# Loads of the first modulation, the entry into attention, and sums behind it, in a two-layer streaming encoder

## The chip, the cores and the metric

The kernel is one program on one core of a Trainium2 chip. A core has TensorE (matmuls, results into PSUM banks), VectorE (DVE in the profile), ScalarE (ACT), GpSimd (POOL) and SyncE (SP, which only issues transfers here), each with its own queue of instructions that run in order, and 16 DMA engines that move data between HBM and the on-chip memory. Transfers are issued from the queues of SP, ACT and POOL. The metric is the device time of one execution in microseconds; lower is better.

## The reference

One inference step of a two-layer encoder on 1024 prompt tokens and 8 samples of 16 tokens, width 1024, float32. All tokens are handled as one batch of 1152 columns; data lie feature-major (128 partitions x 8 feature groups x tokens).

```
mod = silu(c) @ w_ada[l] + b_ada[l]                 # six parts: shift, scale, gate, twice
h   = rms_norm(x, norm_mix[l]) * (1 + scale) + shift
layer 0: RWKV-7 time mixing of h
   xr, xw, xk, xv, xa, xg = h + (h_prev - h) * mix[0..5]
   decay from tanh(xw @ w1) @ w2;  a from (xa @ a1) @ a2;  g from sigmoid(xg @ g1) @ g2
   recurrent state per head over time, group norm, bonus, times g, then @ w_o
layer 1: attention over bands of 9 chunks of 64, shared keys and values made after layer 0,
   q = rms_norm(h @ wb_q) per head;  softmax(q k / 8 + bias[relative distance]);  @ wb_o
each layer then: x = x + gate * SwiGLU(rms_norm(x) * (1 + scale) + shift)
```

Returned are the outputs, the shifted rows and states of layer 0, and the new keys and values.

## The kernel before, in words

Instructions are emitted by Python generators, and a planner of the tile framework then orders them for each engine: it simulates the time line with its own costs, keeps data dependencies and the tiles' reuse, and writes a fixed order per engine and per transfer queue. A tile belongs to a tag with a number of buffers; asking for one more than there are makes the next writer wait until an earlier one is released. `issue_after(ins)` puts the instructions of a block that run on the engine of `ins` behind `ins` in that order. Nearly every product is made in two parts for accuracy: `split` (L271 to L273) writes a rounded high part on ACT and the remainder on DVE, and `mm3` issues three matmuls, high x high, high x low and low x high.

*Beginning.* `setup` loads parameters and constants. `win_open` (L748) opens the pool of the recurrent part, loads the small table `T` (L753), and fills two scratch arrays `Z` in HBM with zeros (L760, four transfers). `proj(0)` (L522) then makes the first block of 384 tokens (408 columns with the shifted rows): `proj_h` (L432) loads the block `hb` (L434), sums squares over the 8 feature groups (ACT L439, DVE L441), forms `rstd` and multiplies (DVE L454), and scales and shifts each feature on ACT (L455). Scale and shift come from `ada_steps` (L201): a unit is four loads of 128 x 1024 weights (`wload`, L260), 16 matmuls on 32-wide quarters of the array, a copy (L222), four small matmuls and an addition (L228). Units 0 and 2 serve features 0 to 3, units 1 and 3 features 4 to 7; `proj_h` runs 8 steps, two units, before features 0 and 4. The weights go to tiles of the recurrent part that are still unused. The list `early` has 14 of them (YL, BKT, UV and XL three each, BK, pa); the 16 loads and the 4 copies of the sums take them in turn, twice round. After all eight features L462 clears column 0 of the block.

Then come the products of `proj_lora` (L574). The first, `wa1`, runs 48 matmuls: all eight features of the current rows, then all eight of the previous rows. Its weights are loaded on POOL's queue and mixed on DVE (`lora_weights`, L390 and L392); the two mixed tiles are also stored to HBM for the later blocks (L396, issued from ACT). They sit in tag `raw`, which has three buffers and also serves `g1a`, the next product.

*Attention.* `kv` makes keys and values and the first two of eight queries (`head`); in the second, scratch comes from `slot(1)`, a ring of 14 buffers of 1280 columns that holds much else. `attention` (L1634) goes over eight pairs of heads. For pair n the generator `queries(n + 2)` (L1720) loads the query weights in halves (L249, raw data in `slot(1)`), splits them and makes a query in four parts, woven between the score tiles; `pair` (L1734) first prepares keys and queries of pair n + 1 (`kprep` L1624, `qprep` L1631), then loads values and bias (L1744). `head_norm` uses two tiles of tag `ht` for each part, of five buffers. Output of two score tiles is copied from PSUM into tile `o`, one buffer (L1833), and stored (L1834).

*Projection behind attention.* `attproj` (L1910) multiplies by `wo` in eight steps of 640 columns, and between the steps `strassen_in` (L1286) prepares the first 512 columns of the feed-forward part: normed features, splits, and 16 sums or differences of 128 x 256 (L1299), which run on GpSimd here.

Of the kernel before, what the change touches and what calls it, by code (L numbers as in the profile page):

```python
# [8 lines left out]
F32 = mybir.dt.float32  # L9
# [136 lines left out]
class Trunk:  # L146
# [54 lines left out]
    def ada_steps(self, units, tag="aux", bufs=1, tile=None):  # L201
# [3 lines left out]
        def load(u, i):  # L205
            w = (tile or self.rawtile)()
            self.wload(w[:, :1024], self.a["wada"][u, i])
            return w
        todo = [(u, i) for u in units for i in range(4)]
        ahead = None  # L210
        for u in units:
            ps = self.bank(tag, bufs)
            for i in range(4):
# [3 lines left out]
                for q in range(4):  # L217
                    mm(nc, ps[32 * q:32 * q + 32, c], self.scT[:, i % 2 * 4 + q, :], w[:, q * 256:q * 256 + 256], i % 2 == 0, i % 2 == 1)
                if i < 3:
                    yield  # L220
            sb = (tile or self.rawtile)()[:, :512]
# [37 lines left out]
    def wload(self, out, src):  # L259
        (self.wqueue or self.nc.sync).dma_start(out, src)  # L260
# [120 lines left out]
    def lora_weights(self, n):  # L381
# [12 lines left out]
        for t in (raw, m):  # L394
            dt = self.dp.tile([128, c], F32, name=self.nm("lw"))
            nc.scalar.dma_start(dt, t[:, :c])  # L396
# [35 lines left out]
    def proj_h(self, b):  # L432
# [15 lines left out]
        for f in range(8):  # L448
# [6 lines left out]
            nc.scalar.activation(x[:, :n], x[:, :n], AF.Identity, scale=self.A0[f][:, 0:1], bias=self.mod[:, f, 0:1])  # L455
            if b == 2:
# [4 lines left out]
        if b == 0:  # L461
            nc.vector.memset(hb[:, :, 0:1], 0.0)  # L462
# [59 lines left out]
    def proj(self, b):  # L522

        if b == 0:
            self.lw = {}
            ring = (f() for _ in range(2) for f in self.early)
            self.ada = self.ada_steps((0, 2, 1, 3), "acc", 2, lambda: next(ring))
            self.A0 = [self.cp.tile([128, 9], F32, name=f"A0_{f}") for f in range(8)]
            self.proj_h(0)
            self.wqueue = self.nc.gpsimd  # L530
# [43 lines left out]
    def proj_lora(self, b, hi, lo):  # L574
# [5 lines left out]
        def first(n, rows):  # L580
            pw = self.bank("acc", 2)
            W = self.lora_in(n)
            for i, (h, l) in enumerate(((hc, lc), (hp, lp))):
                for k in range(8):
                    s = slice(k * rows, (k + 1) * rows)
                    self.mm3(pw[:rows, :TB], W[i][0][:, s], W[i][1][:, s], h[k], l[k], i + k == 0, i + k == 8)
# [161 lines left out]
    def win_open(self, ctx):  # L748
# [4 lines left out]
        nc.sync.dma_start(self.T.rearrange("p c i -> p (c i)"), self.a["ti"])  # L753
        self.Z = [self.dp.tile([64, 32, 64], F32, name=f"Z{i}") for i in range(2)]
        z = self.wt("y", [128, 512])
        nc.gpsimd.memset(z, 0.0)
        for i in range(2):
            zf = self.Z[i].rearrange("c g i -> (c g i)").rearrange("(u p x) -> u p x", u=2, p=128)
            for u in range(2):
                nc.sync.dma_start(zf[u], z)  # L760
        f4 = lambda t: t.rearrange("p a b c d -> p (a b c d)")
        f3 = lambda t: t.rearrange("p a b c -> p (a b c)")
        self.early = [lambda: f4(self.wt("YL", [128, 2, 2, 4, 64], 3))] * 3 + [lambda: f3(self.wt("BKT", [128, 2, 2, 256], 3))] * 3 + \
# [802 lines left out]
    def kv(self, H, X, end):  # L1566
# [40 lines left out]
        for n in range(2):  # L1607
            if n:
                self.evt = lambda tag: self.slot(1)
# [376 lines left out]
```

## Time and profile before

| quantity | value |
|---|---|
| time, median of three runs | 3811.97 us (3804.54 to 3815.72) |
| the profiled execution's own time | 3804.49 us |
| its span | 3802.7 us |
| TensorE busy, weight loads | 3506.1 us, 3098.0 us |
| VectorE, ScalarE, GpSimd busy | 2263.6, 1573.8, 591.6 us |
| mean granted TensorE clock | 0.94 |
| moved by DMA | 554.01 MB, 146 GB/s on average |

All times in the views are microseconds from the start of the span. A row of a time line gives start, duration, engine, line, operation, output and inputs, and in brackets the idle time ahead of it and what ended it. A row of waits gives total, count and longest. A row of groups gives busy time, mean nanoseconds of one, and the idle time ahead. A row of stretches gives, for each engine, busy time and number of instructions, then the granted clock, the DMA share and GB/s. The wide multiplications have one line, L143; they are told apart by their output: `acc`, `S`, `PT` and `O` are banks of PSUM.

### The profile page before, as it was taken

The page shows a single profiled execution, that of the slowest core. Times are in us where ns is not written, and L with a number is a line of the kernel's source. Part 1 is how long each engine was busy: PE and PEld are TensorE (multiplying, and loading weights), DVE is VectorE, ACT ScalarE, POOL GpSimd, SP SyncE. Part 2 cuts the span into 40 slices and gives each one's busy share as a digit, 9 for nine tenths or more (in the row PEclk, how much of TensorE's full clock was granted, in tenths as well). Part 3 has the DMA queues.
Part 4 walks back from the last instruction along what each step waited for, and adds up shares of the span by engine and source line. Part 5 has one row for each costly group of instructions (what it writes and reads, how often), then busy time and mean ns, then how long its engine had stood idle before and what let it go on. Part 6 is the DMA issues. An engine that isn't in the chain of part 4 may idle for free.

```text
span 3802.7 us, 72100 instructions
## 1 busy us (share of the span) xinstructions
PE 3506.1 (92%) x28550; PEld 3098.0 (81%) x28550; DVE 2263.6 (60%) x4396; ACT 1573.8 (41%) x3006; POOL 591.6 (16%) x497
## 2 busy tenths in 40 slices
PE   5889989989999799999999899789889799999999
PEld 4777778777667699999888879667677799999898
DVE  4666667765445854554457742666565755545667
ACT  5545546544223533333311452556554533333310
POOL 0000000000011154453000100000000255444000
PEclk9887899899699899999999999899899899999999
DMA  5876776776665322224654122554565322222521
GB/s 212 236 216 170 207 220 184 201 203 201 192 197 176 113 84 76 76 73 157 221 177 172 64 71 92 153 151 155 152 203 178 120 78 71 76 75 96 171 86 66
DMA packets 426995, 554.01 MB, mean 146 GB/s; under 512 B 128385, under 2 KB 292737, under 8 KB 422177
## 3 DMA queue, kind: packets, MB, share of 16 engines
q1 hardware_dynamic: 351344, 450.68, 36.9%
q0 software_dynamic: 22224, 80.36, 6.9%
q10 hardware_dynamic: 53088, 18.36, 2.1%
q8 instruction: 225, 3.69, 0.4%
q14 instruction: 114, 0.93, 0.1%
HBM read 415.85 MB, written 133.40 MB: 144 GB/s over the span
## 4 chain that ended last, share of the span: by engine, by line
PE 69%; DMA 11%; DVE 10%; issue 4%; ACT 4%; SPq 1%; ACTq 0%; POOL 0%; DVEq 0%; POOLq 0%
PE S L143 32%; PE PT L143 15%; PE acc L143 12%; PE st L143 3%; PE O L143 2%; PE G L143 1%; DVE h L273 1%; PE aux L143 1%; PE PT L1811 1%; PE Y L143 1%; DMA TT<-Z 1%; DMA h<-out_kT 1%; DVE wlo L273 1%; DMA raw<-in_rw_o 1%; DMA h<-in_wo 1%
## 5 line engine op out<-in xcount | busy, mean ns | idle before, releaser
L143 PE MATMUL S<-h,w 128*128 128x320 f32 (+1 forms) x4944 | 689.7, 298 | 12.3 <-ACT h L272 4.8
L143 PEld LDWEIGHTS S<-h,w 128*128 128x128 f32 x4944 | 671.8, 191 | 18.4 <-ACT h L272 5.6
L143 PE MATMUL S<-h,wh 128*128 128x320 f32 (+1 forms) x2844 | 529.8, 338 | 15.9 <-DVE h L1170 6.8
L143 PE MATMUL acc<-mx,whi 128*128 128x384 f32 x1728 | 508.5, 372 | 32.7 <-ACT whi L272 13.0
L143 PEld LDWEIGHTS S<-h,wh 128*128 128x128 f32 x2844 | 456.1, 189 | 70.8 <-issue 12.3
L272 ACT ACTIVATE w<-rq 128x512 fp32r<-128x512 f32 x308 | 192.6, 629 | 515.1 <-PE S L143 201.1
L143 PEld LDWEIGHTS acc<-mx,whi 128*128 128x128 f32 x1728 | 337.6, 204 | 63.3 <-ACT whi L272 16.9
L273 DVE TENSOR_TENSOR w<-rq,w 128x512 fp32r<-128x512 f32 x308 | 267.8, 872 | 199.8 <-ACT w L272 199.0
L143 PE MATMUL PT<-h,w 128*128 128x320 f32 (+1 forms) x2448 | 347.6, 297 | 10.2 <-ACT h L272 4.7
L143 PEld LDWEIGHTS PT<-h,w 128*128 128x128 f32 x2448 | 332.1, 190 | 12.2 <-ACT h L272 5.1
L143 PE MATMUL acc<-mx,wlo 128*128 128x384 f32 x864 | 316.1, 366 | 8.3 <-DVE wlo L273 8.3
L1369 POOL TENSOR_TENSOR t<-t,t 128x576 f32<-128x576 f32 (+1 forms) x132 | 226.5, 1717 | 442.2 <-ACT t L1376 320.1
L143 PE MATMUL PT<-h,wh 128*128 128x320 f32 (+1 forms) x1428 | 284.2, 342 | 8.2 <-ACT h L1558 2.3
L143 PEld LDWEIGHTS PT<-h,wh 128*128 128x128 f32 x1428 | 231.7, 188 | 38.5 <-issue 5.0
L143 PEld LDWEIGHTS acc<-mx,wlo 128*128 128x128 f32 x864 | 175.0, 203 | 20.6 <-DVE wlo L273 12.9
L273 DVE TENSOR_TENSOR wlo<-raw,whi 128x1024 fp32r<-128x1024 f32 x114 | 139.1, 1221 | 84.9 <-ACT whi L272 83.8
L272 ACT ACTIVATE wh<-rq 128x512 fp32r<-128x512 f32 x124 | 74.8, 625 | 245.1 <-PE S L143 161.4
L273 DVE TENSOR_TENSOR h<-h,h 128x1024 fp32r<-128x1024 f32 (+4 forms) x112 | 122.3, 1106 | 88.3 <-ACT h L272 72.1
L272 ACT ACTIVATE whi<-raw 128x1024 fp32r<-128x1024 f32 x114 | 119.6, 1053 | 129.0 <-PE acc L143 62.6
L272 ACT ACTIVATE h<-h 128x1024 fp32r<-128x1024 f32 (+4 forms) x112 | 103.5, 935 | 159.8 <-DMA h<-sd 111.1
L1369 DVE TENSOR_TENSOR t<-S,t 128x576 f32<-128x576 f32 (+1 forms) x116 | 86.4, 744 | 122.7 <-PE S L143 122.7
L1436 DVE TENSOR_TENSOR h<-h,S 128x640 f32<-128x640 f32 (+1 forms) x150 | 111.9, 750 | 78.9 <-PE S L143 78.7
(444 smaller groups left out, 5625.0 us busy)
## 6 DMA issues: line engine op xcount, KB each, us to landing
h<-in_wada SPq DMA_DIRECT2D x64, 512.0 KB, 6.3
rq<-in_wg SPq DMA_DIRECT2D x88, 256.0 KB, 2.6
rq<-in_wu SPq DMA_DIRECT2D x88, 256.0 KB, 2.6
rq<-in_wd SPq DMA_DIRECT2D x88, 256.0 KB, 3.1
raw<-in_wada POOLq DMA_DIRECT2D x32, 512.0 KB, 5.0
kc<-in_ck SPq DMA_DIRECT2D x16, 1024.0 KB, 5.1
vc<-in_cv SPq DMA_DIRECT2D x16, 1024.0 KB, 6.0
sd<-t SPq DMA_DIRECT2D x88, 160.0 KB, 1.9
```

Source lines behind the costliest of these rows:

```text
L143: return nc.tensor.matmul(out, lhsT, rhs, start=start, stop=stop)
L272: self.nc.scalar.activation(hi, x, AF.Copy)
L273: self.nc.vector.tensor_tensor(lo, x, hi, ALU.subtract)
L1369: eng.tensor_tensor(out, x, y, ALU.add)
L1436: nc.vector.tensor_tensor(y, y, d, ALU.add)
L1811: nc.tensor.transpose(pt[:, j * 128:(j + 1) * 128], P[:, j * 128:(j + 1) * 128], self.C("ident"))
```

## The change

In the beginning, the zero fill of `Z` and the load of `T` move into a new function `win_fill`, called after `proj_h(0)` and put behind the last modulation load on SP. Every modulation load has a tile, or two half tiles, of its own: the list `early` becomes an iterator over 12 full tiles of the old tags, two pairs of half tiles (tails of the XL tiles, and `gl`) and the tiles BK and pa; the copies of the sums go to four tiles TT. The two stores of `wa1`'s mixed weights are issued from SP behind the last modulation load, no longer from ACT. Column 0 is cleared feature by feature, and `wa1` of the first block takes features 0 to 3 of current and previous rows first, then features 4 to 7.

In attention, the weights of the third query are loaded in one transfer ahead of the second query's work and split in `queries(2)`; the ACT instructions of `kprep` and `qprep` in `pair` stand behind that split. Output copies take tiles of tag `ht`, which has six buffers in place of five; tag `o` is gone. In `attproj` the 16 sums run on VectorE.

```diff
@@ -198,14 +198,18 @@
             next(self.ada, None)

-    def ada_steps(self, units, tag="aux", bufs=1, tile=None):
+    def ada_steps(self, units, tag="aux", bufs=1, tile=None, sbt=None):

         nc = self.nc

         def load(u, i):
             w = (tile or self.rawtile)()
-            self.wload(w[:, :1024], self.a["wada"][u, i])
-            return w
+            if not isinstance(w, tuple):
+                w = w[:, :1024],
+            n = 1024 // len(w)
+            for j, t in enumerate(w):
+                self.last_load = self.wload(t, self.a["wada"][u, i][:, j * n:(j + 1) * n])
+            return [t[:, o:o + 256] for t in w for o in range(0, n, 256)]
         todo = [(u, i) for u in units for i in range(4)]
@@ -215,10 +219,10 @@
                 c = slice(i // 2 * 256, i // 2 * 256 + 256)
                 for q in range(4):
-                    mm(nc, ps[32 * q:32 * q + 32, c], self.scT[:, i % 2 * 4 + q, :], w[:, q * 256:q * 256 + 256], i % 2 == 0, i % 2 == 1)
+                    mm(nc, ps[32 * q:32 * q + 32, c], self.scT[:, i % 2 * 4 + q, :], w[q], i % 2 == 0, i % 2 == 1)
                 if i < 3:
                     yield
-            sb = (tile or self.rawtile)()[:, :512]
+            sb = sbt() if tile else self.rawtile()[:, :512]
             nc.scalar.activation(sb, ps, AF.Copy)
@@ -257,7 +261,7 @@

     def wload(self, out, src):
-        (self.wqueue or self.nc.sync).dma_start(out, src)
+        return (self.wqueue or self.nc.sync).dma_start(out, src)

@@ -393,7 +397,11 @@
         for t in (raw, m):
             dt = self.dp.tile([128, c], F32, name=self.nm("lw"))
-            nc.scalar.dma_start(dt, t[:, :c])
+            if n == "wa1":
+                with self.tc.issue_after(self.last_load.ins):
+                    nc.sync.dma_start(dt, t[:, :c])
+            else:
+                nc.scalar.dma_start(dt, t[:, :c])
             self.lw[n].append(dt)
@@ -453,13 +461,13 @@
             nc.vector.tensor_tensor(x, x, r, ALU.mult)
             nc.scalar.activation(x[:, :n], x[:, :n], AF.Identity, scale=self.A0[f][:, 0:1], bias=self.mod[:, f, 0:1])
+            if b == 0:
+                nc.vector.memset(x[:, 0:1], 0.0)
             if b == 2:
                 xs = x[:, n:].rearrange("p (b n) -> p b n", n=17)
                 bc = lambda t: t.rearrange("p (b o) -> p b o", o=1).broadcast_to([128, 8, 17])
                 nc.vector.tensor_tensor(xs, xs, bc(self.A0[f][:, 1:9]), ALU.mult)
                 nc.vector.tensor_tensor(xs, xs, bc(self.mod[:, f, 1:9]), ALU.add)
-        if b == 0:
-            nc.vector.memset(hb[:, :, 0:1], 0.0)
         if b == 2:
@@ -523,10 +531,11 @@
         if b == 0:
             self.lw = {}
-            ring = (f() for _ in range(2) for f in self.early)
-            self.ada = self.ada_steps((0, 2, 1, 3), "acc", 2, lambda: next(ring))
+            self.ada = self.ada_steps((0, 2, 1, 3), "acc", 2, lambda: next(self.early), lambda: next(self.early_sb))
             self.A0 = [self.cp.tile([128, 9], F32, name=f"A0_{f}") for f in range(8)]
             self.proj_h(0)
+            with self.tc.issue_after(self.last_load.ins):
+                self.win_fill()
             self.wqueue = self.nc.gpsimd
@@ -580,10 +589,14 @@
             pw = self.bank("acc", 2)
             W = self.lora_in(n)
-            for i, (h, l) in enumerate(((hc, lc), (hp, lp))):
-                for k in range(8):
-                    s = slice(k * rows, (k + 1) * rows)
-                    self.mm3(pw[:rows, :TB], W[i][0][:, s], W[i][1][:, s], h[k], l[k], i + k == 0, i + k == 8)
+            sides = (hc, lc), (hp, lp)
+            if b == 0 and n == "wa1":
+                order = [(i, k) for k0 in (0, 4) for i in range(2) for k in range(k0, k0 + 4)]
+            else:
+                order = [(i, k) for i in range(2) for k in range(8)]
+            for i, k in order:
+                s = slice(k * rows, (k + 1) * rows)
+                self.mm3(pw[:rows, :TB], W[i][0][:, s], W[i][1][:, s], sides[i][0][k], sides[i][1][k], i + k == 0, i + k == 8)
             return pw
@@ -750,19 +763,18 @@

         self.T = self.wp.tile([128, 16, 16], F32, name="T")
-        nc.sync.dma_start(self.T.rearrange("p c i -> p (c i)"), self.a["ti"])
         self.Z = [self.dp.tile([64, 32, 64], F32, name=f"Z{i}") for i in range(2)]
-        z = self.wt("y", [128, 512])
+        z = self.z = self.wt("y", [128, 512])
         nc.gpsimd.memset(z, 0.0)
-        for i in range(2):
-            zf = self.Z[i].rearrange("c g i -> (c g i)").rearrange("(u p x) -> u p x", u=2, p=128)
-            for u in range(2):
-                nc.sync.dma_start(zf[u], z)
         f4 = lambda t: t.rearrange("p a b c d -> p (a b c d)")
         f3 = lambda t: t.rearrange("p a b c -> p (a b c)")
-        self.early = [lambda: f4(self.wt("YL", [128, 2, 2, 4, 64], 3))] * 3 + [lambda: f3(self.wt("BKT", [128, 2, 2, 256], 3))] * 3 + \
-            [lambda: f4(self.wt("UV", [128, 2, 2, 4, 64], 3))] * 3 + [lambda: f3(self.wt("XL", [128, 3, 8, 64], 3))] * 3 + \
-            [lambda: f3(self.wt("BK", [128, 8, 2, 64], 1)), lambda: f3(self.wt("pa", [128, 2, 8, 64], 1))]
+        t5 = lambda tag: f4(self.wt(tag, [128, 2, 2, 4, 64], 3))
+        xl = [f3(self.wt("XL", [128, 3, 8, 64], 3)) for _ in range(3)]
+        tt = [self.wt("TT", [128, 8, 64], 6).rearrange("p a b -> p (a b)") for _ in range(4)]
+        self.early = iter([t5("YL") for _ in range(3)] + [f3(self.wt("BKT", [128, 2, 2, 256], 3)) for _ in range(3)] + [t5("UV") for _ in range(3)] +
+                          [t[:, 0:1024] for t in xl] + [(xl[0][:, 1024:1536], xl[1][:, 1024:1536]), (xl[2][:, 1024:1536], self.wt("gl", [128, 512]))] +
+                          [f3(self.wt("BK", [128, 8, 2, 64], 1)), f3(self.wt("pa", [128, 2, 8, 64], 1))])
+        self.early_sb = iter(tt)
         self.zr = self.wp.tile([128, 128], F32R, name="zr")
@@ -771,6 +783,14 @@
             nc.gpsimd.memset(s, 0.0)
             self.S.append(s)
+
+    def win_fill(self):
+        nc = self.nc
+        nc.sync.dma_start(self.T.rearrange("p c i -> p (c i)"), self.a["ti"])
+        for i in range(2):
+            zf = self.Z[i].rearrange("c g i -> (c g i)").rearrange("(u p x) -> u p x", u=2, p=128)
+            for u in range(2):
+                nc.sync.dma_start(zf[u], self.z)

@@ -1606,6 +1626,8 @@
         for n in range(2):
             if n:
+                self.q2 = self.slot(1)[:, :1024]
+                nc.sync.dma_start(self.q2, self.a["wq"][2])
                 self.evt = lambda tag: self.slot(1)
@@ -1636,7 +1658,7 @@
         self.hw = ("wh", "wl", 3)
         self.halfraw = lambda: self.slot(1)[:, :512]
-        self.evt = lambda tag: self.pp.tile([128, 320], F32, tag=tag, name=self.nm(tag), bufs={"xin": 2, "ht": 5}[tag])
+        self.evt = lambda tag: self.pp.tile([128, 320], F32, tag=tag, name=self.nm(tag), bufs={"xin": 2, "ht": 6}[tag])
         self.qbd = at.tile([128, 4, 2, 16], F32, name="qbd")
@@ -1720,7 +1742,15 @@

         nc = self.nc
-        W = self.halves(self.a["wq"][n])
+        if n == 2:
+            W = []
+            for p in range(2):
+                W.append([self.wq.tile([128, 512], F32R, tag=t, name=self.nm("wh"), bufs=3) for t in ("wh", "wl")])
+                raw = self.q2[:, p * 512:(p + 1) * 512]
+                self.q2_split = nc.scalar.activation(W[p][0], raw, AF.Copy)
+                nc.vector.tensor_tensor(W[p][1], raw, W[p][0], ALU.subtract)
+        else:
+            W = self.halves(self.a["wq"][n])
         yield
@@ -1734,8 +1764,9 @@
         nc = self.nc
         if n < 7:
-            self.kprep(n + 1, 0)
-            self.qprep(n + 1, 0)
+            with self.tc.issue_after(self.q2_split.ins):
+                self.kprep(n + 1, 0)
+                self.qprep(n + 1, 0)
         vf = self.att("vf", [128, 8, 128], 2)
@@ -1829,7 +1860,7 @@
         w = O.shape[-1]
         if n < 7:
-            o = self.att("o", [128, 256], 1)
+            o = self.ev("ht")
             nc.vector.tensor_copy(o[:, 0:w], O)
@@ -1916,7 +1947,7 @@
         r = self.sq_done(next(rest))
         t = [self.slot(1)[:, :1024] for _ in range(4)]
-        sub = self.strassen_in(B, x3, r, A, 72, 0, [t[k // 2][:, k % 2 * 512:(k % 2 + 1) * 512] for k in range(8)])
+        sub = self.strassen_in(B, x3, r, A, 72, 0, [t[k // 2][:, k % 2 * 512:(k % 2 + 1) * 512] for k in range(8)], nc.vector)
         st = self.sq_open()
```

## The prediction

> **What bounds the kernel now.** The page first, with the share of each engine.
>
> ```profile
> PE 3506.1 (92%) x28550; PEld 3098.0 (81%) x28550; DVE 2263.6 (60%) x4396; ACT 1573.8 (41%) x3006; POOL 591.6 (16%) x497
> ```
>
> TensorE works 92% of the span, so an edit can only win where TensorE stands still. The change touches three such places: the beginning, the entry into attention, and the projection behind attention. Each is read by itself. First the beginning, as stretches (busy time and count of each engine, granted clock, DMA share, GB/s):
>
> ```profile
> 10.00:20.00 10.00, 1.23 (x12) 0.38 (x16) 0.72 (x1) 0.96 (x1) 0.00 (x0) 1.00 1.03 422
> 20.00:30.00 10.00, 4.75 (x26) 0.95 (x22) 6.35 (x9) 6.11 (x12) 0.54 (x1) 1.00 1.04 415
> 30.00:40.00 10.00, 5.90 (x42) 3.61 (x43) 5.64 (x10) 5.65 (x9) 0.00 (x0) 1.00 0.80 256
> 40.00:50.00 10.00, 7.95 (x79) 4.63 (x79) 3.06 (x11) 4.42 (x8) 0.00 (x0) 1.00 0.54 213
> 55.00:60.00 5.00, 4.26 (x13) 3.86 (x14) 4.83 (x10) 3.31 (x8) 0.00 (x0) 0.56 0.00 0
> 60.00:65.00 5.00, 5.00 (x29) 5.00 (x29) 1.79 (x3) 1.06 (x1) 0.00 (x0) 1.00 0.00 0
> ```
>
> From 10 to 30 us the 16 DMA engines are full (share 1.03 and 1.04, 415 to 422 GB/s) and TensorE is nearly idle: transfers set the pace. From 30 on they are not full (256, 213 GB/s), though modulation weights are still missing. The chain of waits names what stood in line:
>
> ```profile
> 12.00 7.03 DMA lw<-raw
> ...
> 35.67 9.82 DMA YL<-in_wada
> ...
> 51.98 2.59 ACT hb L455 x4
> ...
> 56.43 24.92 PE acc L143 x127
> ```
>
> The last modulation load is issued at 35.67 and lands at 45.5; features 4 to 7 of the first block are scaled from 51.98, and only then does TensorE run without a gap (56.43). Why the last loads are issued so late is in the waits of SP's queue:
>
> ```profile
> SPq L260 <- PE acc L143: 7.3, 2, 3.8
> ```
>
> For 7.3 us SP held a load back because its tile still fed matmuls: 16 loads and 4 copies share 14 tiles.
>
> **The beginning, step by step.** The transfers concerned, with sizes and time to landing, and SP's issues:
>
> ```profile
> YL<-in_wada SPq DMA_DIRECT2D x5, 512.0 KB, 12.4
> BKT<-in_wada SPq DMA_DIRECT2D x4, 512.0 KB, 5.4
> lw<-raw ACTq DMA_DIRECT2D x4, 512.0 KB, 8.2
> hb<-in_xg SPq DMA_DIRECT2D x1, 1632.0 KB, 11.4
> ...
> Z<-y SPq DMA_DIRECT2D x4, 256.0 KB, 8.1
> ```
>
> ```profile
> 2.60 2.14 SPq L760 DMA_DIRECT2D Z<-y  x4
> 4.79 0.59 SPq L434 DMA_DIRECT2D hb<-in_xg  x1
> ```
>
> *Loads.* Moved behind the last load are the zero fill (4 x 256 KB), the small table T and the two stores of wa1's mixed weights (2 x 512 KB). The two stores of g1a follow by themselves, since their second tile is freed only by wa1's stores. That is 3072 KB, 3.15 MB, at 415 GB/s 7.6 us. The hole from 30 to 40 us (256 of 415 GB/s) is worth 10 x (1 - 256/415) = 3.8 us, and closes because every load has a tile of its own (two are split in halves, so SP issues two more, under 0.5 us each, and its queue has room). Sum 11.4 us: the last load lands at 34.1, and L455 starts on feature 4 at 51.98 - 11.4 = 40.6.
>
> A sentence apart: the Trainium skill, "DMA: Bandwidth & Descriptors", section "Issuing engines are not separate DMA queues", says that transfers of all issuing engines run on the same 16 engines and interleave, so another queue saves issue time only; a share of 1.03 here agrees. By it the move of wa1's stores from ACT to SP brings nothing, and only their place behind the loads does; were they to interleave all the same, 2.5 us of the 11.4 would be lost.
>
> *The first block's norm.* hb is issued 2.2 us earlier (the four fills ahead of it are gone: 2.60 to 4.79), so it lands at 14.0 instead of 16.2. ACT no longer sits in the issue of wa1's stores (12.00 to 19.03 in the chain).
>
> ```profile
> 20.95 0.53 ACT L439 ACTIVATE nacc<-hb 128x408 f32<-128x408 f32 x1
> ...
> 38.09 4.04 DVE L454 TENSOR_TENSOR hb<-hb,rstd 128x408 f32<-128x408 f32 x8
> ...
> 66.27 0.34 PE L143 MATMUL acc<-mx,wlo 128*128 128x384 f32 x1
> ```
>
> The squares can start between 14 and 16 instead of 20.95; with 6 us taken, the product with rstd starts at 32.1 instead of 38.09. The modulation of features 0 to 3 needs the first 8 loads, 8 x 512 KB or 10.1 us ahead of the last: 24.0, and with the same 6.5 us from landing to L455 (45.5 to 51.98) 30.5. The norm is the later one. Product (4.04/8), scaling (2.59/4) and a split like it add 1.8 us: first matmul at 33.9.
>
> *Matmuls.* The new order and the clearing of column 0 per feature let 24 of wa1's 48 matmuls run on features 0 to 3 alone. At the clock of 55 to 60 us (0.56; 13 in 4.26 us, 0.33 each) they take 7.9 us: until 41.8, just when feature 4 is split (40.6 + 1.2). The other 24 need 4.1 us at the full clock (29 in 5 us, 0.172 each); the four scalings and splits of ACT take some 4.6. End near 47, or 50 if the clock is low throughout. Before, the end was 66.27 + 0.34 = 66.6. That is 16.5 to 19.5 us; **I take 18**. Upper bound 23: first half done before feature 4 comes and the loads at 422 GB/s from the start. Lower bound 11 (the first rival). Behind it nothing else is late: g1a's weights need wa1's stores landed (34.1 + 2.1 MB of fill and stores at 415 GB/s, 39.2) and 2.4 us on DVE, before 47. The cover is 5 us; without it each us later is a us lost. Eight small memsets for one cost under 0.1 us each.
>
> A sentence apart: the Trainium skill, "TensorE: Matmul & The Clock Gate", section "What's actually happening", says that the clock is halved until about 3.4 us of sustained work and falls back after an idle window. The rows of 0.56 and 1.00 agree; by the rule an earlier but starved first half leaves the second half slow, which speaks against the split: 16.5 in place of 18.
>
> **Entry into attention.** TensorE, ACT alone, and SP's wait:
>
> ```profile
> 2427.79 0.80 PE L143 MATMUL acc<-h,wh 128*128 128x256 f32 x2 [8.13 <-ACT wh L272]
> ```
>
> ```profile
> 2420.76 0.47 ACT L332 ACTIVATE h<-h 128x320 f32<-128x320 f32 x1
> 2426.17 1.06 ACT L272 ACTIVATE h<-h 128x1024 fp32r<-128x1024 f32 x1 [4.93 <-DMA h<-out_kT]
> 2427.13 1.13 ACT L272 ACTIVATE wh<-h 128x512 fp32r<-128x512 f32 x2
> ```
>
> ```profile
> SPq L249 <- DVE h L334: 9.3, 1, 9.3
> ```
>
> TensorE waits 8.13 us for the third query's weights: SP holds their load 9.3 us for a free slot, and ACT then splits them behind the next pair's keys (2426.17). With the load before the second query's work and the keys' splits put behind (queued behind the new wait are ACT's splits for pair 1, which nobody needs before pair 1), the weights can be split when ACT is done with the norms (2420.76 + 0.47 = 2421.2), so matmuls start about 2422.5 instead of 2427.79: 5 us. Bounds: 8 if ACT finds an earlier gap, 0 if the softmax of the first tiles, which this does not move, sets the pace and the matmuls only wait elsewhere. **I take 5**, since 24 matmuls fill an empty stretch. The early load takes one ring slot in place of two; that hides in SP's own wait.
>
> *Output scratch.*
>
> ```profile
> PE O L143 <- DVE o L1833: 4.4, 2, 2.3
> ```
>
> ```profile
> 2556.02 0.35 DVE L1745 TENSOR_SCALAR bt<-bt 128x256 f32<-128x256 f32 x1 [3.44 <-DMA bt<-in_rel]
> ```
>
> At most 4.4 us, but the copy came late because DVE stood ahead of it at a bias load (3.44), not for want of scratch: **0**, bounds 0 to 4.4.
>
> **Sums on VectorE.** Groups from 2944 to 2978 us, then single rows:
>
> ```profile
> L273 DVE TENSOR_TENSOR h<-h,h 128x256 fp32r<-128x256 f32 x28 | 13.9, 554 | 2.1 <-ACT h L272 2.1
> L1299 POOL TENSOR_TENSOR h<-h,h 128x256 f32<-128x256 f32 x12 | 12.7, 1086 | 574.6 <-DVE h L273 574.6
> ```
>
> ```profile
> 2952.17 1.43 DVE L273 TENSOR_TENSOR h<-h,h 128x256 fp32r<-128x256 f32 x4
> ```
>
> ```profile
> 2972.08 7.81 PE L143 MATMUL S<-h,wh 128*128 128x320 f32 x34 [4.82 <-DVE wh L273]
> ```
>
> A DVE operation of this size takes 0.36 us alone (1.43/4), 0.55 on average beside POOL. Sixteen sums on DVE cost 16 x 0.36 = 5.8 us; 28 splits back at 0.36 give 28 x 0.19 = 5.4. DVE's total hardly changes; POOL's 1.09 us a sum leaves the chain. TensorE stood 4.82 us because DVE was late. Bounds: 6 (the stall and some low clock after it), -3 (sums ahead of the weights' low halves). **I take 3.**
>
> **Sum.** 18 + 5 + 0 + 3 = 26 us. The profiled execution ran 3804.49 us, its span and what lies around it, 7.5 under the median of the runs shown; 3804.5 - 26 = 3778.5 for it, and 3812 - 26 = **3786** for a median.
>
> **Rivals.**
> 1. *The stores hold up DVE.* In the same tiles g1a's mixing comes on DVE; planned ahead of the product with rstd, it blocks DVE until wa1's stores have landed (39.2 + 2.4 = 41.6). The norm then is later than before, first matmul 43.4, first half until 51.3, the second until 55.4: 11 us instead of 18. For it: DVE runs in a fixed order. Against: the planner sees the store's new place. 3812 - 19 = 3793.
> 2. *Only the beginning counts.* Attention waits for its bias and DVE's total stays: 3812 - 18 = 3794. For it: 0 and 3 above are soft.
> 3. *Slower: the norm's scratch ring clogs.* Output tiles now sit in ring ht until SP has stored them, and ACT's squares of the query norms need that ring.
>
> ```profile
> DMA to landing us min/median/max: 1.6/2.1/9.7
> ```
>
> If each of the 24 norms waits for one store, 24 x 2.1 = 50 us come on top: 3786 + 50 = 3836. It decides once a store takes longer than six allocations; a pair of some 57 us makes 13, so 26 us. Against it: 9.7 at most.
> 4. *No change.* The planner orders the untouched middle anew and loses about what was won: 3800 to 3815. No row prices that; the three runs alone spread over 11 us.
>
> **Numbers.** Forecast 0.56 (own range 3774 to 3798: 14 to 37 us), rival 1 0.13, rival 2 0.15, rival 3 0.06, rival 4 0.10. Range 3770 to 3806: it drops rival 3, most of rival 4 and a little below. 0.3% is 11.4 us, about what a measurement of this kernel can tell. Faster: 0.56 + 0.11 + 0.13 + 0.02 = 0.82; same 0.11; slower 0.07.
>
> **What would show it.** Right: full DMA until about 34 us, first block matmul near 34, wa1 done near 47 to 50; SP free of waits for matmuls there; no ACT wait for lw. In attention the 8.13 us gap under 4; behind it no POOL sums and no 4.8 us stall. Wrong: DVE's L390 waiting for lw at 35 to 40, ACT waiting at L1522 for og stores, wa1 done after 56, or a middle stage longer by more than 5 us.

## The result, and the profile after

The changed kernel takes 3853.0 us (median; 3840.9 to 3858.5) where the kernel before takes 3813.8 us beside it: ratio 1.0102, 95% interval 1.0085 to 1.0119. **The change makes the kernel 1% slower.** The forecast was 3786 us, 0.7% faster. The profiled execution of after has a span of 3851.6 us, 48.9 more than that of before. Its busy times, from the page:

```profile
PE 3535.0 (92%) x28550; PEld 3120.8 (81%) x28550; DVE 2269.7 (59%) x4419; ACT 1571.4 (41%) x3006; POOL 566.9 (15%) x481
```

TensorE runs the same 28,550 instructions and is busy 28.9 us longer with them. Nothing was added to it; its instructions take longer on average, and it also stands longer.

To see where, the two traces are laid side by side by their transfers: the same transfer is issued in both, so the difference of its two issue times says how far after has fallen back by then. From these differences each kernel is cut at the same points of its work (50 us of before to a point, the median of the transfers there). Lengths in us:

| stage of before | before | after | difference |
|---|---|---|---|
| 0 to 400 (beginning; from 50 us on the shift stays) | 400 | 382 | -18 |
| 400 to 1150 (first projections and windows; no line is edited) | 750 | 797 | **+47** |
| 1150 to 2400 (no line is edited) | 1250 | 1251 | +1 |
| 2400 to 2900 (attention) | 500 | 527 | **+27** |
| 2900 to 3000 (projection behind attention) | 100 | 93 | -7 |
| 3000 to the end | 803 | 802 | -1 |

So the edits won what they were meant to win in two places, and twice as much and more went elsewhere. One profiled execution against another leaves up to some 20 us of chance in a stage (kernels that keep before's order of the second stage, below, take 746 to 765 us for it), so the table shows where to look; the sizes come from the timed runs.

**The beginning** came out as worked out. Stretches of after (us; busy time and instructions of TensorE, its weight loads, VectorE, ScalarE and POOL; granted clock, share of the DMA engines, GB/s):

```profile
10.00:20.00 10.00, 5.91 (x43) 1.61 (x43) 7.29 (x10) 5.85 (x10) 0.00 (x0) 1.00 1.01 410
20.00:30.00 10.00, 7.31 (x53) 3.65 (x52) 1.36 (x3) 6.43 (x10) 0.00 (x0) 1.00 1.03 400
30.00:40.00 10.00, 7.72 (x77) 5.30 (x77) 9.25 (x27) 6.40 (x12) 0.23 (x1) 1.00 0.81 316
40.00:50.00 10.00, 8.83 (x48) 8.02 (x48) 7.05 (x18) 6.13 (x10) 0.31 (x1) 1.00 0.30 119
```

and single rows of its timeline (start, duration):

```profile
32.07 4.03 DVE L462 TENSOR_TENSOR hb<-hb,rstd 128x408 f32<-128x408 f32 x8
...
36.76 0.45 PE L143 MATMUL acc<-mx,whi 128*128 128x384 f32 x1 [1.90 <-ACT mx L276]
...
40.93 0.64 DVE L461 TENSOR_SCALAR A<-mod,par 128x9 f32<-128x9 f32 x4
...
49.17 0.35 PE L143 MATMUL acc<-mx,wlo 128*128 128x384 f32 x1
```

The norm's product starts at 32.07 (38.09 before), wa1's first matmul at 36.76, its 48th ends at 49.5 instead of 66.6. The clock is full throughout.

**The untouched stage.** The same stage in before and in after, one row each:

```profile
400.00:1150.00 750.00, 685.84 (x7882) 558.60 (x7881) 464.42 (x1066) 355.91 (x704) 50.84 (x97) 0.89 0.70 202
```

```profile
382.00:1179.00 797.00, 706.33 (x7842) 575.88 (x7840) 464.55 (x1062) 355.86 (x711) 50.11 (x96) 0.85 0.67 191
```

VectorE and ScalarE do the same work in the same time. TensorE stands 797 - 706.3 = 90.7 us instead of 64.2, 26.5 more, and is busy 20.5 more (the stage holds 40 matmuls fewer, since the new order moves some across the cuts; over the whole kernel both have 28,550), at a clock of 0.85 instead of 0.89: 47 in all. The two halves go together. The trace gives the clock in windows of 3.41 us; 68 of this stage's are at the low clock in after, 50 in before, in 20 spells instead of 17, and 17 of the 20 begin behind a window in which TensorE stood for more than 40% (11 of the 17 before). In these 68 windows TensorE is busy 90% of the time on average: a spell mostly begins behind a hole, and then outlasts it. What released TensorE in the holes (us in total, times, longest), before and after (lines of after lie 4 to 31 behind those of before; L699 is before's L686):

```profile
PE aux L143 <- DMA raw<-in_wada: 0.9, 1, 0.9
...
PE aux L686 <- ACT e L680: 0.6, 2, 0.3
```

```profile
PE aux L143 <- DMA raw<-in_wada: 7.9, 7, 2.3
...
PE aux L699 <- ACT e L693: 5.2, 2, 4.4
```

These two rows hold 11.6 of the 26.5 us; the rest is spread over others. The first are the matmuls of the modulation units 4 to 11, fed by loads of POOL's queue that no edit touches. As built, after has every instruction of this stage that before has, in another order on TensorE, VectorE, ScalarE and SP. In the first seven twentieths of its stream TensorE keeps 73 to 95 of 100 pairs of neighbours, ScalarE keeps 17 to 73 in its first nine; behind them, up to attention, both keep 95 and more. The planner fixes the order from times that it simulates, and with another beginning it dealt what follows anew.

**Attention.** Entry and body are two matters. At the entry the 8.13 us wait is gone, and the waits of the next stretch are

```profile
PE PT L1842 <- DVE P L1837: 4.7, 1, 4.7
PE acc L143 <- DVE h L337: 2.1, 1, 2.1
...
PE acc L143 <- DVE wh L1751: 1.3, 1, 1.3
```

8.1 us in these three (L1842 is before's L1811). In the body, before and then after:

```profile
2550.00:2900.00 350.00, 311.62 (x2769) 249.53 (x2764) 224.07 (x649) 203.19 (x464) 0.00 (x0) 0.95 0.54 170
```

```profile
2582.00:2957.00 375.00, 326.05 (x2757) 259.25 (x2758) 229.81 (x647) 202.14 (x464) 0.00 (x0) 0.92 0.51 156
```

again the same work, 10.6 us more standing and 14.4 us more busy at a lower clock (17 low windows in 12 spells, where before has 10 in 5; all 12 begin behind a window in which TensorE stood for more than 40%).

### The profile page after: what moved, and what is told of

It reads as the page before. It is cut to its first block, busy times and chain, and to the rows that moved or that the text cites. A ratio compares the mean times of both kernels' runs of the same rounds, so it can differ in the third digit from the quotient of the medians.

```text
span 3851.6 us, 72088 instructions
## 1 busy us (share of the span) xinstructions
PE 3535.0 (92%) x28550; PEld 3120.8 (81%) x28550; DVE 2269.7 (59%) x4419; ACT 1571.4 (41%) x3006; POOL 566.9 (15%) x481
```

## The experiments

Ratios are to the kernel before, run beside each. Two theories are open at the start: the losses are the work of the new *order*, or of what the edits *leave behind* (tiles, transfers, ring places).

### Which part brings which stage

The beginning's edits alone, **e1_start**: all of the diff that lies ahead of attention.

```diff
+                self.last_load = self.wload(t, ...)      # a tile or two halves for each modulation load
...
+                with self.tc.issue_after(self.last_load.ins):
+                    nc.sync.dma_start(dt, t[:, :c])      # wa1's stores; T and Z likewise in win_fill
...
+                order = [(i, k) for k0 in (0, 4) for i in range(2) for k in range(k0, k0 + 4)]
```

> The edits of the beginning alone; attention and the sums stay as before. In the two profiles the time until 400 us fell by about 17 us, and the stages from 400 to 1150 us, which no edit touches, grew by about 46 us. Theory A (the beginning's edits bring both): 3814 - 17 + 46 = 3843 us, ratio 1.008, with the stages from 400 to 1150 us longer by 40 to 50 us. Rival (the loss in the middle belongs to the other edits, or differs from build to build): 3797 us, ratio 0.9955, and those stages as long as before.

Measured: 3829.7 us, ratio 1.0052 (1.0035 to 1.0069). The first 400 us are 18 shorter, the untouched stage takes 812 us in the profiled execution, which ran 15 us above the median. The beginning's edits bring both the gain and the loss in the middle; the expectation was 13 us too high.

The sums alone, **e4_sums**:

```diff
-        sub = self.strassen_in(B, x3, r, A, 72, 0, [...])
+        sub = self.strassen_in(B, x3, r, A, 72, 0, [...], nc.vector)
```

> The kernel before with the seven sums of the attention projection on VectorE, and nothing else. In the two profiles the stretch from 2900 to 3000 us of before became 7.4 us shorter. Theory: 3814 - 7.4 = 3806.5 us, ratio 0.998. Forecast of the prediction: 3 us, ratio 0.999. Rival (the shorter stretch came from the other edits in attention, which reach it with work already done): 3814 us, ratio 1.000.

Measured: 3807.8 us, ratio 0.9985 (0.9974 to 0.9995), 5.7 us by the ratio; the stretch of 100 us takes 93. (The sums are 16, not the seven of the expectation.) The interval shuts out the rival's zero, so the gain is the sums' own; it doesn't tell 3 us from 7.4. The waits of TensorE in that stretch, before and here:

```profile
PE S L143 <- DVE wh L273: 4.8, 1, 4.8
PE S L143 <- ACT wh L272: 1.8, 1, 1.8
```

```profile
PE S L143 <- ACT wh L272: 1.3, 1, 1.3
PE S L143 <- DVE wh L273: 0.7, 1, 0.7
```

4.6 us of waiting go, and with the hole the low clock behind it: 0.95 becomes 1.00 in the stretch, and TensorE is busy 87.4 instead of 89.7 us.

### Order or edits: the middle

Both runs carry a table, applied when the program is traced. It ties every instruction behind wa1's first product to the one that is to stand ahead of it on its engine or queue (23,007 on TensorE, 4,188 on VectorE, 2,959 on ScalarE, 489 on POOL, 1,894 on SP); an edge fixes the order of issue and adds no wait.

```diff
         Trunk(tc, a, o).build()
+        pin_order(nc, tc)      # for each engine: every instruction of the table behind the one listed ahead of it
```

**e2_start_old_order**: the beginning's edits, the rest in the order of before.

> The same edits of the beginning, and a table that makes every engine and queue issue all that is traced behind the first block's first LoRA product in the order in which the kernel before issues it; the table adds order and no waits. Theory A1 (the loss in the middle is the new order in which the planner put it): the middle is as long as before and the gain of the beginning stays, 3814 - 17 = 3797 us, ratio 0.9955. Rival A2 (the loss is what the edits leave behind: other tiles under the rotating buffers, fills and stores that land later): as without the table, 3843 us, ratio 1.008.

Measured: 3796.8 us, ratio 0.9963 (0.9946 to 0.9981).

**e3_old_start_new_order**: no edit at all, the rest in the order that the planner chose for e1.

> The kernel before with none of the edits, and a table that makes every engine and queue issue all that is traced behind the first LoRA product in the order that the planner chose for the kernel with the beginning's edits. A1: the whole loss of the middle without the beginning's gain, 3814 + 46 = 3860 us, ratio 1.012. A2: as before, 3814 us, ratio 1.000, or a few us more for an order made for another beginning.

Measured: 3847.8 us, ratio 1.0088 (1.0072 to 1.0104). Its stage and the waits in it:

```profile
408.00:1202.00 794.00, 707.30 (x7886) 575.89 (x7885) 465.44 (x1064) 357.08 (x711) 50.32 (x96) 0.85 0.67 191
```

```profile
PE aux L146 <- DMA raw<-in_wada: 8.7, 8, 2.6
```

This settles it. With the old order the edits' gain is there whole (14 us of 3811), and without any edit the new order alone costs 34 us (46 were expected) and shows after's clock, busy time and waits. The two multiply to 0.9963 x 1.0088 = 1.0051, and e1 is 1.0052: tiles, fills and late stores left behind have no part that can be measured, which with these intervals means less than some 11 us.

### Does every new order lose?

Three parts of the beginning's edits, each with whatever order the planner gives it. **e10_fill**: only T and Z behind the load that is traced last; the order behind the beginning stays.

```diff
+            with self.tc.issue_after(self.last_load.ins):
+                self.win_fill()
```

> The kernel before with T's load and Z's fill queued behind the last modulation load, and nothing else; behind the beginning the planner keeps its order here (99 to 100 of 100 neighbouring pairs on TensorE, VectorE and ScalarE stay neighbours behind the first tenth). By the prediction's price for moved bytes, 7.6 us for 2.1 MB, of which T and Z are 1.1 MB: 4 us, 3807 us, ratio 0.999. Theory A1: a gain and no loss, since nothing is re-ordered. Rival: a loss although the order stays, which would speak against A1.

Measured: 3809.2 us, ratio 0.9991 (0.9977 to 1.0004): no loss, and a gain (3.4 us by the ratio) that can be told neither from none nor from the 4 us expected. The edit moves less than it seems: in the planner's order of SP's queue four of the 16 loads still come behind Z. And ScalarE still issues the lw stores, which wait for VectorE's mixing with other work behind them:

```profile
26.91 1.86 SPq L778 DMA_DIRECT2D Z<-y  x4
30.84 0.84 SPq L260 DMA_DIRECT2D XL<-in_wada  x2
32.05 1.35 SPq L260 DMA_DIRECT2D YL<-in_wada  x2
```

```profile
38.48 0.42 ACT L1036 ACTIVATE UV<-S 64x256 f32<-64x256 f32 x1 [7.30 <-DVE raw L390]
```

So the norm's product starts at 32.84 instead of 38.09, but feature 4 is scaled at 56.06, no earlier than before (51.98). **e11_tiles_fill**: a tile for each load, and T and Z behind; the lw stores stay on ScalarE's queue and wa1's matmuls in their old order.

```diff
+            self.ada = self.ada_steps((0, 2, 1, 3), "acc", 2, lambda: next(self.early), lambda: next(self.early_sb))
...
+                self.win_fill()
```

> A tile for each modulation load, and T and Z behind them, without the LoRA stores and wa1's new order of matmuls. The planner leaves the middle's beginning nearly as it was and re-orders from some 500 us on. Theory A3 (any new order of the middle loses, since before's is a good one): the loads' part of the gain, some 11 us, against a loss of 25 to 36 us: 3830 us, ratio 1.005. Rival A4 (each re-ordering is another draw, better or worse): anything from 3797 to 3840 us, ratio 0.9963 to 1.008.

Measured: 3843.2 us, ratio 1.0082 (1.0064 to 1.0100). **e12_wa1_order**: only wa1's new order of matmuls and the clearing feature by feature.

```diff
+                order = [(i, k) for k0 in (0, 4) for i in range(2) for k in range(k0, k0 + 4)]
...
+                nc.vector.memset(x[:, 0:1], 0.0)
```

> The kernel before with wa1's matmuls in the new order and column 0 cleared feature by feature, with every transfer as before. The loads still bound the beginning, so by the prediction it gains 0 to 4 us there; the planner re-orders all the middle. A3: the loss of e3, 3811 + 33 = 3844 us, ratio 1.0088. A4: another draw, from 3800 to 3850 us, ratio 0.997 to 1.010.

Measured: 3839.3 us, ratio 1.0069 (1.0048 to 1.0091). The untouched stage takes some 780 us in e11 and e12. In the profiled executions of the nine kernels that keep before's order of it (e2, e4 to e8, e10, and e13 and e14 below) it takes 746 to 765 us, in before 750; in the five with new orders (after, e1, e3, e11, e12) some 780 to 812, and 787 in e9 below. The five are three orders, since after, e1 and e3 issue this stage alike on TensorE and ScalarE. So none of the three was as good as before's; that none could be is not shown, and e12's 26 us fits both of its theories. e12 is the clearest warning: it gains nothing in its first 400 us (402), and re-orders 750 us that it doesn't touch.

e11 also says which part the beginning's gain hangs on: its first 400 us are 415 long. ScalarE's rows there:

```profile
29.29 0.36 ACTq L400 DMA_DIRECT2D lw<-raw  x1
29.70 0.54 ACT L443 ACTIVATE ntmp<-hb 128x408 f32<-128x408 f32 x1 [13.68 <-DMA XL<-in_wada]
31.99 0.34 ACTq L400 DMA_DIRECT2D lw<-raw  x1
```

The norm's fifth square stands 13.68 us behind the fourth, in the queue behind the issue of an lw store; what releases it is the landing of a modulation load. In the program as built the store waits for a completion counter that it shares with just that load (XL, landed at 29.21), so it is the program that makes it wait. The loads come without a pause and the norm later than before. With the stores moved to SP and wa1's new order as well (e1, e2) the gain is there; the two were not tried one by one.

### What in the new order costs

**e9_start_old_modulation_steps**: e1 with 66 edges on TensorE that put the modulation matmuls of the middle back between their old neighbours; in the planner's order nearly all stand 15 to 200 matmuls later.

```diff
+    for first, then in STEPS:          # 66 pairs of TensorE's instructions, counted from the end
+        tc.add_manual_dep(mine[-then], mine[-first].name, info, reason="pin_steps")
```

> The edits of the beginning with the planner's own order, as in e1, except that 66 pairs put TensorE's matmuls of the modulation units 4 to 11 (the scT products between 750 and 1200 us) back between the neighbours that they have in the kernel before; in the new order nearly all of them stand 15 to 200 matmuls later. The order before them stays new. Theory C (a good part of the loss lies in these steps: TensorE waits 7.9 to 8.7 us for their weights where it waited 0.9, and each wait of some 2 us leaves the clock low behind it): 15 to 20 us less than e1, ratio 1.0052 - 0.0045 = 1.001, 3813 us. Rival (they are only where the late work shows; the loss is in the order of the rest): as e1, ratio 1.005.

Measured: 3815.5 us, ratio 1.0006 (0.9987 to 1.0026), 0.0046 less than e1. The wait for their weights:

```profile
PE aux L143 <- DMA raw<-in_wada: 2.6, 3, 1.2
```

About half the price of the new order (17.5 us, some 8 to 27 by the intervals) goes with these 66 edges on 128 small matmuls. But they aren't all that changed: with them the planner also dealt the other engines anew (in two twentieths of ScalarE's stream 37 and 38 of 100 pairs of e1's neighbours are left, in two of VectorE's 43 and 46), so what the place of the 128 alone is worth isn't shown. The wait itself is 2.6 us against 5.2 in e1's profile and 7.9 in after's, so most of the gain isn't this wait itself; nor did the clock fall behind each such wait, as theory C had it (in after soon behind two of the five of over 0.6 us). The profiled execution of e9 lies 13 us above its median and shows 787 us for the stage, so where in the stage the rest came from isn't read from it. The other half, the distance from e9 to e2 (0.0043), was not split further.

### Attention: ring, order, third weight

**e5_ring**: the output scratch in ring ht, six buffers for five.

```diff
-            o = self.att("o", [128, 256], 1)
+            o = self.ev("ht")
```

> The kernel before with the output scratch in the ring ht (six buffers for five) and nothing else. What the changed kernel lost in attention is, from the ratios of the runs so far, 1.0102 / 1.0052 / 0.9985 = 1.0065, some 25 us, for the scratch's ring and the third query weight together. Theory B (the ring edit has nearly all of it): 3811 + 20 to 25 = 3834 us, ratio 1.006. Rival (the loss is the third query weight's, whose edit makes ScalarE's key and query halves queue behind its split): 3811 us, ratio 1.000. The prediction had 0 for the ring.

Measured: 3836.0 us, ratio 1.0074 (1.0050 to 1.0097). **e6_old_scratch_ring_order**: scratch and ring of before, and a table like e3's with e5's order.

> The kernel before with its own single scratch tile and five buffers, and a table that makes every engine and queue issue in the order which the planner chose for the ring edit. Theory B1 (order): as slow as the ring edit itself, 3834 us, ratio 1.006. Rival B2 (the prediction's third rival: norms wait in the ring for stores of the outputs): 3811 us, ratio 1.000, since no output lies in the ring here.

Measured: 3847.3 us, ratio 1.0088 (1.0067 to 1.0109): no faster without any output in the ring, so the loss is again the order, and the clogged ring (the prediction's third rival) is out. Nor is it the single scratch tile under a foreign order: TensorE waits 0.9 us for o there, and its long waits are e5's (14.4 us for so, 8.4 for the samples' pts). The reverse, the ring edit in before's order, was not run. **e7_third_query_weight**:

```diff
+                self.q2 = self.slot(1)[:, :1024]
+                nc.sync.dma_start(self.q2, self.a["wq"][2])
...
+            with self.tc.issue_after(self.q2_split.ins):
+                self.kprep(n + 1, 0)
+                self.qprep(n + 1, 0)
```

> The kernel before with the third query weight loaded early and split without the ring of halves, and the key and query halves of a pair queued behind that split; nothing else. The prediction: the 8.13 us gap at the entry goes, - 5 us, 3806 us, ratio 0.9987. Theory B: 3806 to 3811 us, ratio 0.9987 to 1.000. Rival: + 20 to 25 us, 3834 us, ratio 1.006.

Measured: 3812.4 us, ratio 0.9997 (0.9982 to 1.0012). No gain can be told, though the interval, -7 to +5 us of time, doesn't shut out the forecast's -5. The trace shows why little is left: the wait for the weight at the entry went, and 4.9 us behind VectorE's probabilities came in its place, as in after.

What of e5's order costs? TensorE's longest waits in the body of attention, before and in e5:

```profile
PE PT L1811 <- ACT pts L1812: 14.3, 19, 4.2
...
PE PT L1811 <- DVE so L1906: 4.2, 8, 0.7
```

```profile
PE PT L1811 <- DVE so L1906: 14.1, 10, 2.9
PE PT L1811 <- ACT pts L1812: 9.6, 17, 0.9
PE PT L1811 <- ACT pts L1890: 8.9, 4, 2.4
...
PE acc L143 <- DVE ht L333: 2.9, 3, 1.0
```

The sample groups stand out (so, and pts of L1890): the projection's matmuls, which in before stand between them and so can cover their short chain, come some 27 places later in e5, the tiles' some 18 earlier. Two runs tried to give the cover back, with edges like e9's on top of e5: **e13_ring_old_sample_steps** with 96 and **e14_ring_old_cover** with 48.

> The ring edit of e5 with the planner's own order, except that 96 pairs put TensorE's output matmuls and transposes of the 14 sample groups back between the neighbours that they have in the kernel before. In e5 the 350 transposes of the tiles wait 14.1 us for the sample outputs (so) where they waited 4.2, and 8.9 us for the samples' weights (pts of L1890) where they waited 1.3; TensorE stands some 12 us longer in attention and is some 12 us longer at the low clock. Theory D (the place of the sample groups between the projection's matmuls carries the loss): 10 to 20 us less than e5, ratio 1.003, 3821 us. Rival D2 (the order of all the tiles against the projection carries it): as e5, ratio 1.0074, 3838 us.

> The ring edit of e5, with 48 pairs that only keep the last projection matmul (h by wh) which stood ahead of each run of sample instructions ahead of it again: the samples come later, their neighbours behind them stay as the planner has them. Theory D: less of the gain than e13, since what follows a sample group still waits for it: ratio 1.004 to 1.006, 3825 to 3833 us. Rival D2: as e5, ratio 1.0074.

Measured: 3849.6 us, ratio 1.0108 (1.0091 to 1.0125), and 3857.3 us, ratio 1.0120 (1.0101 to 1.0140). Neither gains anything on e5, and e14 is slower: theory D falls in the form of these edges. In e13:

```profile
PE acc L143 <- DVE ht L333: 18.0, 7, 4.0
PE PT L1811 <- DVE so L1906: 12.1, 9, 2.9
...
PE PT L1811 <- ACT pts L1890: 3.0, 4, 1.6
```

The wait for the samples' weights fell from 8.9 to 3.0, the one for their outputs hardly, and the key and query norms (ht) now hold TensorE 18.0 us instead of 2.9. The edges moved the hole. They also moved more than the samples: of e5's neighbours on ScalarE only 59 to 95 of 100 are left in four twentieths of its stream in attention and behind it, on VectorE 65 to 94 in five. That the order carries attention's loss is shown (e6); which part of it does stays open.

### A version that beats both

**e8_start_sums_old_order**: the beginning's edits and the sums, the rest held by a table like e2's in the order planned for the sums alone; attention's edits are left out.

> The edits of the beginning and the sums on VectorE together, without the two edits in attention, and a table that keeps the order which the planner chose for the sums alone behind the first LoRA product. If the two gains add (0.9963 x 0.9985 = 0.9948): 3811 - 20 = 3791 us. If the sums' 3.4 us depend on what came before them: 3797 us, ratio 0.9963.

Measured: 3787.0 us, ratio 0.9933 (0.9913 to 0.9953). The gains add: 0.9963 x 0.9985 = 0.9948 lies in the interval. This is the number of the forecast, reached without the two edits in attention and with the order held. That it meets 3786 so closely is in part luck, since the two parts measured by themselves make 20 us, not 26.

## Why the prediction was wrong

Point by point, by its own steps.

- **Beginning, 18 us: right.** -16 to -19 in the profiles from 50 us on, 14 (7 to 21) by e2. Norm product 32.1, came at 32.07; modulation of features 4 to 7 from 40.6, came at 40.93; wa1's end 47 to 50, came at 49.5, 17.1 us before the old one (the seven other runs with before's beginning end wa1 at 68.8 to 71.4, so before's 66.6 was an early one). One step in it was off: first matmul 33.9, came at 36.76, since ScalarE did three more scalings and two mixing copies ahead of the first split; the second half bounds the end, so it cost nothing. The price of the moved bytes by themselves (4 us for T and Z) is not tested: e10 moves them ahead of four loads still to come, and ScalarE's store issue stands in the way. In what was run the gain came only with the tiles, the moved stores and wa1's order together. The first rival (VectorE held up by the stores) did not come.
- **The clock in wa1's second half.** The Trainium skill ("TensorE: Matmul & The Clock Gate", "What's actually happening") would have allowed a half clock there, 16.5 us instead of 18. The rows of after from 30 to 50 us show 1.00, so it was not needed; in e2 the clock from 40 to 50 us is 0.83 and wa1 ends at 50.6.
- **Entry into attention, 5 us: no gain to be told** (e7: -7 to +5 us of time). The wait named did go. The step that failed is "what is late next": 4.9 us behind VectorE's P at the next transposes, and the second query's own norm and split, which the prediction did not name. Its lower bound, 0, is nearest to what came, though the timed runs don't exclude the 5.
- **Output scratch, 0: wrong, +28 us** (19 to 37 by e5). The step priced the waits for the scratch, and these did stay small, as it said (3.1 us in e5, 4.4 in before's row); it did not price that an edit to a ring changes when the planner finds a place free, and with that the order of all attention.
- **Sums, 3 us: right in kind, rather small in size**, 5.7 (2 to 10, which still holds the 3), with 7 in the stretch. The prediction put the stall of 4.82 us and "some low clock after it" into its bound of 6 and took half; the waits lost 4.6 us and the low clock was worth another 2.3 of TensorE's busy time. VectorE's operations took 0.42 us there, not the 0.36 reckoned with (e4), and that cost nothing.
- **The sum.** 18 + 5 + 0 + 3 has no term for the 750 us between, and here the prediction failed: each edit was costed where it stands, and the planner was taken to leave the rest alone. The premise at its head, that an edit can only win where TensorE stands still, hides the other side: 28.9 of after's 48.9 us are TensorE's busy time, longer for the same matmuls. The fourth rival named just this, and failed twice: its size (3800 to 3815, a loss of 14 to 29 us; e3 measures 34 for the middle alone, e5 another 28 for attention) and its chance, 0.10. With "No row prices that" a cost without a row seems to have been taken for a small one. Of its signs of being wrong only the last came: a middle stage longer by over 5 us.

From the parts: 1.0052 (e1) x 1.0074 (e5) x 0.9997 (e7) x 0.9985 (e4) = 1.0108, against 1.0102 measured for the whole. Nothing is left over that these intervals could tell.

## What to carry to other kernels

Where one planner orders the whole program, an edit is not local: before costing it, look how many neighbours each engine's stream keeps, and where it keeps fewer, put tens of us beside the edit's own few (those dealt anew in e3, e5, e11 and e12 left the kernel 26 to 34 us slower). Measure an edit with the old order held by edges that add no waits; the loss of a new order can then be told from the edit's gain, and the gain be had without it. And a hole on TensorE can cost more than its length, since matmuls behind it may run at a low clock (2.3 us beside 4.6 of waiting in e4).

## What the runs showed of the hardware

**Being busy was not enough to restore the clock.** From before's trace, a stretch of 51 us and some groups in it (instructions, busy us, mean ns):

```profile
967.00:1018.00 51.00, 44.98 (x268) 30.98 (x268) 24.11 (x65) 11.65 (x22) 2.65 (x5) 0.50 0.70 190
```

```profile
L143 PE MATMUL G<-XL,BK 64*128 64x128 f32 x55 | 12.5, 420 | 5.2 <-DMA BK<-sp_k 5.2
L143 PE MATMUL acc<-mx,whi 128*128 128x384 f32 x16 | 10.1, 657 | 0.0
...
L143 PE MATMUL st<-UV,XL 128*64 128x64 f32 x32 | 4.7, 331 | 0.0
...
L143 PE MATMUL st<-TT,p 32*32 32x32 f32 x32 | 2.1, 237 | 0.0
```

TensorE is busy 45.0 of the 51 us and has the clock at 0.50 all the time; its full-size matmuls take 657 ns where they take 372 on average over the kernel, so the record is real. The Trainium skill ("TensorE: Matmul & The Clock Gate", "What's actually happening") lets the clock rise after some 3.4 us of sustained work. The trace's clock does change in steps of 3.41 us, but of before's 86 windows at the low clock in which TensorE was busy for nine tenths or more, only 45 were followed by the full clock. Counting instead the columns streamed, each weighted with the active part of the array, as a share of what full-size matmuls stream at the low clock: with 0.7 and more, 36 of 39 low windows were followed by the full clock, with less than 0.3, 1 of 36 (of the 86 busy ones alone: 33 of 33, 1 of 10, and 11 of the 43 between); and at the full clock 838 of 839 windows with 0.7 and more kept it, with less than 0.3 none of 25. That is a count over one trace (after's is alike: 41 of 41 and 0 of 42 for the low windows), not an experiment.

**Short holes bring the low clock too.** Of TensorE's holes that began at the full clock in after, 26 of the 29 of 2 to 3.4 us were followed by the low clock within some 5 us, 23 of the 50 of 1 to 2 us, and 25 of the 89 of 0.3 to 1 us (in before 21 of 28, 18 of 39, 18 of 93). Together the two counts fit the losses: a hole starts a low spell, and small matmuls behind it keep the spell going. No run tests that by itself.
